# A two-block transformer on one core: where the halves of weights and their operands begin in SBUF, modulo 512 bytes

## The chip, the core and the metric

One core of a Trainium2 chip runs the whole program in one launch. The metric is the device time of that core in microseconds, shorter is better. Before the change three runs took 3350.55, 3352.53 and 3353.84 us; their median is 3352.53 us.

## What is computed

Two blocks over 512 tokens of 2048 features, in float32. The first projects the normalised input to queries, keys, values and gates, runs a differential attention of 8 heads and a state space branch, and merges both through gates. The second has two layers, each with a neighbourhood attention (6 heads), a dilated attention (6 heads) and an attention to 256 memory tokens (4 heads).

```python
def first_block(x, ...):
    h = rms_norm(x, ln_gain[l]);  proj = h @ w_in[l]
    q, k, v, z_att, u, z_ssm, g_att, g_ssm = jnp.split(proj, splits, axis=-1)
    ...
    merged = (jax.nn.sigmoid(g_att) * (y_att @ w_proj_att[l])
              + jax.nn.sigmoid(g_ssm) * (y_ssm @ w_proj_ssm[l]))
    x = x + merged @ w_out[l]

def second_block(x, mem, ...):
    for l in range(DEPTH_2):
        z = rms_norm_2(x, norm_g[l]) @ w_in[l]
        ...
        mk, mv = jnp.split(mem_n @ w_mem_kv[l], 2, axis=-1)
        ...
        x = x + y @ w_out[l]
    return rms_norm_2(x, final_g)
```

Nearly all the work is in these products with weight matrices.

## The kernel before

**Products in three matmuls.** A float32 operand is split into two halves, high and low, that are each exact in the type float32r, and a product is the sum of three: high by high, high by low, low by high. `mm3` (L174 to L179) issues them; L177, L178 and L179 are the three lines at which nearly every matmul of the trace stands.

```python
    def mm3(self, ps, wh, wl, xh, xl, start, stop):
        mm = self.nc.tensor.matmul
        mm(ps, wh, xh, start=start, stop=False)
        mm(ps, wh, xl, start=False, stop=False)
        mm(ps, wl, xh, start=False, stop=stop)
```

The first operand is loaded into the array as the stationary one (128 columns of 4 bytes: 512 bytes of each partition), the second streams past it as the moving one. In a row of the trace the moving tile stands before the stationary one.

**Weights.** `wunit` (L186) brings a unit of weights, 4 k tiles by 256 columns (512 KB), by a DMA to a tile `raw`, and `split` (L181) makes the halves `hl`: ScalarE casts (L183), VectorE subtracts (L184). There are 3 buffers of each, and the units are issued up to 5000 instructions ahead of their place.

```python
            hl = (pool or self.wh).tile([P, 2, 4, 256], FR, tag="hl", ...)[:, :, :kk, :cw]
            self.split(hl[:, 0], hl[:, 1], raw)
```

**Three kinds of product.** `gemm_t` (L215) makes two tiles [128 columns of weights, 512 tokens]: the halves of weights are stationary and the operand moves, 512 columns. For the memory (`memory_kv`, L333) the same function has 256 tokens and so 256 moving columns. `gemm_tok` (L226) makes tiles [128 tokens, 256 columns of weights]: the operand is stationary and the halves of weights move, 256 columns. Both call `accumulate` (L237), which goes over the k tiles and calls `wunit`. Between the matmuls, steps of attention and of the state space branch are spread (`push`, `tick`).

**Where tiles begin.** Pools are laid one behind the other from the bottom of SBUF (left) or from its top (right). The order and sizes in `__init__` (L116 to L134) put the buffers of `raw` and `hl` at 96 bytes past a multiple of 512 in each partition, the left pools that follow at 160 past one, and the right pools at 480 past one. A slice of an operand begins a multiple of 512 bytes into its tile (128 columns are 512 bytes, a row of 512 tokens 2048, the low half follows the high one by 1024, 2048 or 4096), so all slices of a kind have one place modulo 512:

| operand | pool | before | after |
|---|---|---|---|
| halves of weights, `gemm_t` over 512 tokens | `wh` | 96 | 256 |
| halves of weights, `gemm_t` over the memory | `wh` | 96 | 64 |
| halves of weights, `gemm_tok` | `wh` | 96 | 448 |
| the same, last 256 columns of the program | `fin`, right | 480 | 448 |
| operands of the first block's input and last products, and of the second block's output products | `xg1`, `mrg`, `y2`, left | 160 | 0 |
| operands of the memory, of the gated unit, of the merge and of the second block's input products | `memx`, `glu`, `y1`, `xg2`, `xg3`, right | 480 | 0 |

What the text calls the **distance** is how far the stationary tile begins past the moving one, modulo 512:

| kind of product | matmuls | distance before | after |
|---|---|---|---|
| `gemm_t`, 512 columns, operand in a left pool | 4992 | 448 | 256 |
| `gemm_t`, 512 columns, operand in a right pool | 5184 | 128 | 256 |
| `gemm_t`, 256 columns (memory) | 384 | 128 | 64 |
| `gemm_tok`, operand in a left pool (first block's values, last product) | 2112 | 64 | 64 |
| `gemm_tok`, operand in a right pool (memory's and second block's values) | 2688 | 384 | 64 |
| `gemm_tok`, last 256 columns | 192 | 192 | 64 |

The counts are those of the program: 96 matmuls for each `gemm_t` of 16 k tiles, 48 for one of 8.

Of the kernel before, what the change touches and what calls it, by code (L numbers as in the profile page):

```python
# [8 lines left out]
F32 = mybir.dt.float32  # L9
# [7 lines left out]
P = 128  # L17
# [9 lines left out]
# column starts of the first block's input projection  # L27
Q0, K0, V0, ZA0, U0, ZS0, GA0, GS0 = 0, 1024, 2048, 3072, 4096, 5120, 6144, 8192
# column starts of the second block's input projection
# [3 lines left out]
# key tiles that a tile of queries attends to in the neighbourhood attention  # L33
NA_LO = (0, 0, 1, 2)
NA_N = (2, 3, 3, 2)
# the first of the 32 grid columns that it sees
NA_COL = (0, 8, 24, 32)

# instructions by which the loads and splits of weights go ahead of their place
AHEAD = 5000  # L40
AHEAD_FIRST = 180
# k tiles of a product between two steps of other work
# [27 lines left out]
def shape_constants():  # L70
    """Arrays that depend on shapes alone."""
# [10 lines left out]
    # rows of a tile of queries: 16 grid columns by 8 grid rows  # L82
# [27 lines left out]
def natural(ap):  # L110
    """Tokens of a tile in the second block's order, viewed in their natural order."""
    return ap.rearrange("p (c r) -> p r c", r=8)


class Net:
    def __init__(self, ctx, tc, a):  # L116
# [9 lines left out]
        nc.vector.memset(self.onesD, 1.0 / D)  # L126
        self.wr = ctx.enter_context(tc.tile_pool(name="wr", bufs=3))
# [3 lines left out]
        self.col = ctx.enter_context(tc.tile_pool(name="col", bufs=16))  # L131
# [4 lines left out]
    # ---- small helpers  # L136
# [9 lines left out]
    def exact(self, key):  # L146
        """A constant exact in float32r."""
        t, x = self.cp.tile([P, P], FR, name="r_" + key), self.t512(P)
        self.load(x, self.a[key])
        self.nc.scalar.copy(t, x)  # L150
        return t
# [22 lines left out]
    def mm3(self, ps, wh, wl, xh, xl, start, stop):  # L174
        """wh, wl are the exact halves of one operand, xh, xl of the other one."""
# [5 lines left out]
    def split(self, hi, lo, src):  # L181
        """src = hi + lo, both exact in float32r."""
        self.nc.scalar.copy(hi, src)  # L183
        self.nc.vector.tensor_sub(lo, src, hi.bitcast(F32))  # L184

    def wunit(self, src, k0, kk, c0, cw=256, pool=None):  # L186
        with self.tc.high_priority(self.ahead):
            raw = self.wr.tile([P, 4, 256], F32, tag="raw", name=self.nm("raw"))[:, :kk, :cw]
            self.nc.sync.dma_start(out=raw, in_=src[k0 * P:(k0 + kk) * P, c0:c0 + cw].rearrange("(k p) c -> p k c", p=P))
            hl = (pool or self.wh).tile([P, 2, 4, 256], FR, tag="hl", name=self.nm("hl"), bufs=4 if pool else 3)[:, :, :kk, :cw]  # L190
# [3 lines left out]
    def push(self, steps, every):  # L194
        """Spread the steps of a generator over the products that follow: one every so many k tiles,
        or as many as the step before gives."""
# [18 lines left out]
    def gemm_t(self, src, c0, mov, n=T):  # L215
        """Two tiles [128 columns of src, n tokens]; mov: halves [128, 2, n] of each k tile."""
# [7 lines left out]
        return self.accumulate(src, c0, len(mov), out, step)  # L224

    def gemm_tok(self, src, c0, mov, nt):  # L226
        """nt tiles [128 tokens, 256 columns of src]."""
# [7 lines left out]
        return self.accumulate(src, c0, len(mov), out, step)  # L235

    def accumulate(self, src, c0, kt, out, step):  # L237
        """The products over all k tiles; in the first unit of weights the tiles start two by two,
        in the last one they end one after another."""
        n = len(out)  # L240
        for ku in range(0, kt, 4):
            hl = self.wunit(src, ku, 4, c0)
# [10 lines left out]
    def exp_tables(self, after):  # L253
        """Logarithm and exponential from one table, to be loaded after an instruction."""
# [3 lines left out]
    def rsqrt(self, out, ms):  # L258
        """out = (ms + EPS) ** -0.5, a Newton step behind the activation tables."""
# [10 lines left out]
    def norm_stats(self, acc, n=T, pool=None):  # L270
        """acc: squares summed over the k tiles; rstd along the free axis, and as columns."""
# [8 lines left out]
        cols = self.nrm.tile([P, 4], F32, tag="rcol", name=self.nm("rcol"))[:, :n // P]  # L280
# [11 lines left out]
    def add_squares(self, acc, x, first):  # L292
        """acc += x * x"""
# [7 lines left out]
    def gained(self, hl, x, g):  # L301
        """The halves of x * g, g a column."""
# [4 lines left out]
    # ---- the stages  # L307
    def transposed_in(self, src, nt, pool, hls, gains, stage, acc, spill=None):
        """Rows of src to tiles [128 features, tokens] times the gain, and the squares of the rows, in steps."""
# [23 lines left out]
    def memory_kv(self, hls, row, cols):  # L333
        """Keys [features, memory] and values [memory, features] of both layers, to scratch."""
# [16 lines left out]
    def ssm_params(self, sp):  # L351
        """Discretised transition powers and the input and output maps, states on partitions:
        real parts on the lower half, imaginary parts on the upper one."""
# [43 lines left out]
        # powers, doubling  # L397
# [11 lines left out]
        # (a - 1) / lambda  # L409
# [14 lines left out]
        # input maps (re; im) and (-im; re)  # L424
# [18 lines left out]
        # output maps (re; -im) and (-im; -re)  # L443
# [8 lines left out]
        # transition over a chunk for the scan: (ai; -ai), matched to the swapped halves  # L452
# [5 lines left out]
    def ssm_powers(self, e, ar, ai, k0, m1, m2, g0):  # L458
        """e [states, 16 groups, (8 powers, 16 channels)] = ar^k m1 + ai^k m2, in 8 steps."""
# [12 lines left out]
    def ssm(self, sp):  # L472
        """The state space branch from u_d [feature, (j, chunk)] to yl_d, the same order, in steps.
        Tokens are chunk * 8 + j. The powers of a batch of 16 groups go with the products of the one before."""
# [15 lines left out]
        def every(n, k):  # L490
            """The pace of n products, with a step of what goes beside them at every k-th."""
# [92 lines left out]
    # ---- first block  # L584
    def first(self):
# [11 lines left out]
        with ExitStack() as sx:  # L597
# [27 lines left out]
            with tc.tile_pool(name="ssm", bufs=3, side="right", reuse_waits="tile") as sp:  # L625
                # gates of the merge, with the branch between them
# [77 lines left out]
    def residual(self, xp, xg, acc, o, k, gains, spill):  # L704
        """The next layer's operand from a tile of the residual."""
# [6 lines left out]
    def gate(self, ps, row):  # L712
        """silu(ps * row)"""
# [7 lines left out]
    def gated(self, yp, ps, f):  # L721
        """The halves of o * silu(z), o from scratch."""
# [14 lines left out]
    def ssm_out(self, gp, yt, yh):  # L737
        """Tiles of gelu(y + d u) and their halves, in steps."""
# [520 lines left out]
```

## Time and profile before

| | |
|---|---|
| three runs | 3350.55, 3352.53, 3353.84 us |
| profiled execution | span 3350.6 us; no time outside it is listed |
| TensorE busy with matmuls | 3314.5 us, 99% of the span, 17844 |
| VectorE, ScalarE, GpSimd busy | 1754.8, 1175.0 and 293.0 us |
| granted TensorE clock over the span | 0.998 |
| DMA | 122 GB/s in the mean |

Matmuls are pipelined: a row's duration is longer than the step to the next one (0.39 us against some 0.23 us for 512 columns), so durations and busy shares hardly tell how fast TensorE goes. How many matmuls start in a stretch does: a window's length by their number is the **step**. A window also counts the one or two matmuls that began before it and reach into it, and the step is worked out without two of them.

### The profile page before, as it was taken

To read this page: it belongs to the slowest core of one execution; us is meant where nothing else is said; L and a number is where in the kernel's file an instruction comes from. 1 tells how busy PE (TensorE), PEld (TensorE's weight loads), DVE (VectorE), ACT (ScalarE), POOL (GpSimd) and SP (SyncE) were. 2 spreads that over 40 slices of the span, in tenths; PEclk is the share of its full clock that TensorE was granted. 3 is DMA by queue.
4 is the path that set the end of the run, shared out by engine and by line. 5 is a ranking of instruction groups with operands and counts; after the bars stand their busy time and mean duration, and the time that the engine had idled before them with its cause. 6 is when DMAs were issued, how large, how long until landed. Compare 5 with 4: busy or idle time off the path is not lost.

```text
span 3350.6 us, 44958 instructions
## 1 busy us (share of the span) xinstructions
PE 3314.5 (99%) x17844; PEld 2830.3 (84%) x17844; DVE 1754.8 (52%) x3227; ACT 1175.0 (35%) x1851; POOL 293.0 (9%) x426
## 2 busy tenths in 40 slices
PE   8999999999999999999999999999999999999998
PEld 6998877888888788888888888888888888888898
DVE  5564486445888754444444556443354445554433
ACT  4432222243555432233333334323343333342333
POOL 3200001311111000011011000001100100000000
PEclk9999999999999999999999999999999999999999
DMA  6564434453333354344232222333443222223433
GB/s 224 175 195 119 128 121 121 138 190 121 104 101 101 112 174 144 123 145 144 96 95 94 90 85 73 125 118 133 145 134 98 93 89 89 82 92 119 139 111 114
DMA packets 365954, 410.11 MB, mean 122 GB/s; under 512 B 36506, under 2 KB 327209, under 8 KB 365616
## 3 DMA queue, kind: packets, MB, share of 16 engines
q1 hardware_dynamic: 350800, 363.73, 34.2%
q0 software_dynamic: 14944, 43.52, 4.0%
q8 instruction: 140, 2.29, 0.3%
q14 instruction: 70, 0.57, 0.1%
HBM read 355.86 MB, written 47.70 MB: 120 GB/s over the span
## 4 chain that ended last, share of the span: by engine, by line
PE 94%; DVE 3%; DMA 1%; issue 1%; ACT 0%; POOL 0%; SPq 0%; DVEq 0%; ACTq 0%; POOLq 0%
PE pg L177 29%; PE pg L179 28%; PE pg L178 28%; PE pa L178 1%; PE pa L1124 1%; PE pa L177 1%; PE pa L179 1%; DVE hl L184 1%; DVE s L558 0%; PE pa L576 0%; DMA raw<-in_w_in_dram 0%; DVE s L557 0%; DVE s L559 0%; DVE st L560 0%; DVE s L556 0%
## 5 line engine op out<-in xcount | busy, mean ns | idle before, releaser
L184 DVE TENSOR_TENSOR hl<-raw,hl 128x1024 fp32r<-128x1024 f32 x552 | 680.8, 1234 | 965.2 <-ACT hl L183 963.9
L177 PE MATMUL pg<-xg,hl 128*128 128x512 f32 (+1 forms) x2688 | 1077.8, 401 | 0.0
L179 PE MATMUL pg<-xg,hl 128*128 128x512 f32 (+1 forms) x2688 | 1047.5, 390 | 8.2 <-DVE hl L184 8.2
L178 PE MATMUL pg<-xg,hl 128*128 128x512 f32 (+1 forms) x2688 | 1044.9, 389 | 0.0
L183 ACT CAST hl<-raw 128x1024 fp32r<-128x1024 f32 x552 | 578.7, 1049 | 1105.0 <-PE pg L179 933.2
L179 PEld LDWEIGHTS pg<-xg,hl 128*128 128x128 f32 x2688 | 506.0, 188 | 123.3 <-DVE hl L184 13.0
L177 PEld LDWEIGHTS pg<-xg,hl 128*128 128x128 f32 x2688 | 507.5, 189 | 93.4 <-DVE v L305 1.3
L178 PEld LDWEIGHTS pg<-xg,hl 128*128 128x128 f32 x2688 | 507.8, 189 | 87.7
L177 PE MATMUL pg<-hl,xg 128*128 128x256 f32 x1152 | 328.7, 285 | 0.0
L179 PE MATMUL pg<-hl,xg 128*128 128x256 f32 x1152 | 324.0, 281 | 0.0
L178 PE MATMUL pg<-hl,xg 128*128 128x256 f32 x1152 | 323.4, 281 | 0.0
L177 PE MATMUL pg<-yh,hl 128*128 128x512 f32 x576 | 227.1, 394 | 0.0
L179 PE MATMUL pg<-yh,hl 128*128 128x512 f32 x576 | 226.6, 393 | 0.0
L178 PE MATMUL pg<-yh,hl 128*128 128x512 f32 x576 | 225.6, 392 | 0.0
L178 PEld LDWEIGHTS pg<-hl,xg 128*128 128x128 f32 x1152 | 217.3, 189 | 1.5
L177 PEld LDWEIGHTS pg<-hl,xg 128*128 128x128 f32 x1152 | 217.1, 188 | 1.5
L179 PEld LDWEIGHTS pg<-hl,xg 128*128 128x128 f32 x1152 | 216.9, 188 | 0.0
L184 DVE TENSOR_TENSOR wt<-pa,wt 128x512 fp32r<-128x512 f32 (+3 forms) x144 | 83.0, 576 | 120.8 <-ACT wt L183 120.5
L177 PE MATMUL pg<-hl,yh 128*128 128x256 f32 x512 | 144.4, 282 | 0.0
L178 PE MATMUL pg<-hl,yh 128*128 128x256 f32 x512 | 142.2, 278 | 0.0
L179 PE MATMUL pg<-hl,yh 128*128 128x256 f32 x512 | 142.2, 278 | 0.0
L183 ACT CAST wt<-pa 128x512 fp32r<-128x512 f32 (+3 forms) x144 | 71.3, 495 | 169.5 <-PE pa L1124 168.8
(282 smaller groups left out, 3982.9 us busy)
## 6 DMA issues: line engine op xcount, KB each, us to landing
raw<-in_w_in_dram SPq DMA_DIRECT2D x384, 512.0 KB, 3.6
raw<-in_w_out_dram SPq DMA_DIRECT2D x96, 512.0 KB, 3.6
raw<-in_w_mem_kv_dram SPq DMA_DIRECT2D x32, 512.0 KB, 4.3
o_d<-t POOLq DMA_DIRECT2D x40, 256.0 KB, 2.3
t<-o_d SPq DMA_DIRECT2D x40, 256.0 KB, 3.9
sg_d<-t POOLq DMA_DIRECT2D x32, 256.0 KB, 2.5
raw<-in_w_proj_att_dram SPq DMA_DIRECT2D x16, 512.0 KB, 3.9
raw<-in_w_proj_ssm_dram SPq DMA_DIRECT2D x16, 512.0 KB, 3.6
```

What stands on the lines that cost most here:

```text
L177: mm(ps, wh, xh, start=start, stop=False)
L178: mm(ps, wh, xl, start=False, stop=False)
L179: mm(ps, wl, xh, start=False, stop=stop)
L183: self.nc.scalar.copy(hi, src)
L184: self.nc.vector.tensor_sub(lo, src, hi.bitcast(F32))
L1124: self.nc.tensor.transpose(pt[:, i * P:(i + 1) * P], w, self.ident)
```

## The change

It gives `wunit` a parameter `at`, the place of the halves in a tile that is 512 bytes larger (2176 words instead of 2048), and `accumulate` hands it on: 256 for `gemm_t`, 64 for `gemm_t` over the memory, 448 for `gemm_tok`. The rest makes pools begin at multiples of 512: 88 words of filling among the constants (`fill`), the pool of columns `col` moved ahead of the weights' pools, the two small tiles `rcol` moved to it from `nrm`, and a tile of 120 words (`line`) at the top, ahead of the right pools. Comments and docstrings are gone too, which shifts line numbers by 6 to 9.

```diff
+AT_T, AT_MEM, AT_TOK = 256, 64, 448
...
         nc.vector.memset(self.onesD, 1.0 / D)
+        self.col = ctx.enter_context(tc.tile_pool(name="col", bufs=16))
+
+        line = ctx.enter_context(tc.tile_pool(name="line", bufs=1, side="right"))
+        line.tile([P, 120], F32, name="line")
         self.wr = ctx.enter_context(tc.tile_pool(name="wr", bufs=3))
         self.wh = ctx.enter_context(tc.tile_pool(name="wh", bufs=3))
         self.tmp = ctx.enter_context(tc.tile_pool(name="tmp", bufs=8))
         self.nrm = ctx.enter_context(tc.tile_pool(name="nrm", bufs=2))
-        self.col = ctx.enter_context(tc.tile_pool(name="col", bufs=16))
...
-    def wunit(self, src, k0, kk, c0, cw=256, pool=None):
+    def wunit(self, src, k0, kk, c0, cw=256, pool=None, at=0):
...
-            hl = (pool or self.wh).tile([P, 2, 4, 256], FR, tag="hl", name=self.nm("hl"), bufs=4 if pool else 3)[:, :, :kk, :cw]
+            hl = (pool or self.wh).tile([P, 2176], FR, tag="hl", name=self.nm("hl"), bufs=4 if pool else 3)
+            hl = hl[:, at // 4:at // 4 + 2048].rearrange("p (h k c) -> p h k c", h=2, k=4)[:, :, :kk, :cw]
...
-        return self.accumulate(src, c0, len(mov), out, step)
+        return self.accumulate(src, c0, len(mov), out, step, AT_MEM if n == NMEM else AT_T)
...
-        return self.accumulate(src, c0, len(mov), out, step)
+        return self.accumulate(src, c0, len(mov), out, step, AT_TOK)
...
-            hl = self.wunit(src, ku, 4, c0)
+            hl = self.wunit(src, ku, 4, c0, at=at)
...
-        cols = self.nrm.tile([P, 4], F32, tag="rcol", name=self.nm("rcol"))[:, :n // P]
+        cols = self.col.tile([P, 4], F32, tag="rcol", name=self.nm("rcol"), bufs=2)[:, :n // P]
...
-            hls = [self.wunit(w_out, ku, 4, f * P, pool=fp) for ku in range(0, KD, 4)]
+            hls = [self.wunit(w_out, ku, 4, f * P, pool=fp, at=AT_TOK) for ku in range(0, KD, 4)]
...
         self.lam = cp.tile([P, 1], F32, name="lam")
+        cp.tile([P, 88], F32, name="fill")
```

No instruction is added, removed or moved: on each of the five engines both programs have the same operations on the same tiles in the same order. Of the waits two differ, because buffers of one stage now lie over others of the stage before: one addition of GpSimd (the bias of a neighbourhood attention) no longer waits for TensorE, and the load of the final gain (`fg`, in `last`) also waits for a matmul of the second layer's attention.

## Rows read from the trace of the kernel before

**Rows 1.** The page: span, busy time of the matmul engine, granted clock, the last chain.
```profile
span 3350.6 us, 44958 instructions
PE 3314.5 (99%) x17844; PEld 2830.3 (84%) x17844; DVE 1754.8 (52%) x3227; ACT 1175.0 (35%) x1851; POOL 293.0 (9%) x426
...
PEclk9999999999999999999999999999999999999999
...
PE 94%; DVE 3%; DMA 1%; issue 1%; ACT 0%; POOL 0%; SPq 0%; DVEq 0%; ACTq 0%; POOLq 0%
```

**Rows 2.** Groups by shape, whole span (count, busy us, mean ns), a third of each kind.
```profile
L177 PE MATMUL pg<-xg,hl 128*128 128x512 f32 x2560 | 1041.7, 407 | 0.0
...
L177 PE MATMUL pg<-hl,xg 128*128 128x256 f32 x1152 | 328.7, 285 | 0.0
...
L177 PE MATMUL pg<-yh,hl 128*128 128x512 f32 x576 | 227.1, 394 | 0.0
...
L177 PE MATMUL pg<-hl,yh 128*128 128x256 f32 x512 | 144.4, 282 | 0.0
...
L177 PE MATMUL pg<-m,hl 128*128 128x512 f32 x256 | 100.9, 394 | 0.0
```

**Rows 3.** Windows of 512-column products alone: stretch, length, matmul time (count), clock, DMA.
```profile
1372.00:1532.00 160.00, 160.00 (x701) 1.00 0.42 143
1192.00:1350.00 158.00, 158.00 (x682) 1.00 0.50 159
2100.00:2245.00 145.00, 145.00 (x626) 1.00 0.37 120
2995.00:3135.00 140.00, 140.00 (x604) 1.00 0.37 121
212.20:257.20 45.00, 45.00 (x195) 1.00 0.59 169
```

**Rows 4.** Windows of 256-column products alone, the same columns.
```profile
144.00:166.00 22.00, 22.00 (x188) 1.00 0.69 223
167.00:188.80 21.80, 21.80 (x186) 1.00 0.65 215
1650.00:1672.00 22.00, 22.00 (x186) 1.00 0.30 94
...
3318.00:3339.80 21.80, 21.80 (x187) 1.00 0.32 99
```

**Rows 5.** Timeline, first block's values: first and last of 83 matmuls (start, duration).
```profile
833.69 0.28 PE L177 MATMUL pg<-hl,xg 128*128 128x256 f32 x1
...
842.99 0.28 PE L178 MATMUL pg<-hl,xg 128*128 128x256 f32 x1
```

**Rows 6.** Timeline, last product: first and last of 83 matmuls.
```profile
3195.69 0.36 PE L177 MATMUL pg<-hl,yh 128*128 128x256 f32 x1
...
3205.09 0.28 PE L178 MATMUL pg<-hl,yh 128*128 128x256 f32 x1
```

**Rows 7.** Timeline, all engines, 1430 us: a moving stream and the next load.
```profile
1430.03 0.39 PE L178 MATMUL pg<-m,hl 128*128 128x512 f32 x1
1430.04 0.19 PEld L179 LDWEIGHTS pg<-m,hl 128*128 128x128 f32 x1
```

**Rows 8.** Window of the scan (busy and count by engine), and matmuls' wait in it.
```profile
428.00:536.00 108.00, 100.47 (x429) 79.48 (x427) 100.71 (x362) 21.22 (x26) 7.45 (x11) 1.00 0.38 117
...
PE pg L179 <- DVE hl L184: 7.5, 9, 1.1
```

**Rows 9.** What feeds a unit of weights: groups by line, DMA landing, load of `fg`.
```profile
L184 DVE TENSOR_TENSOR hl<-raw,hl 128x1024 fp32r<-128x1024 f32 x552 | 680.8, 1234 | 965.2 <-ACT hl L183 963.9
L183 ACT CAST hl<-raw 128x1024 fp32r<-128x1024 f32 x552 | 578.7, 1049 | 1105.0 <-PE pg L179 933.2
raw<-in_w_in_dram SPq DMA_DIRECT2D x384, 512.0 KB, 3.6
3151.35 0.42 SPq L154 DMA_DIRECT2D fg<-in_final_g_dram  x1
```

More of the change, by code (lines that the diff above doesn't have):

```diff
@@ L233, in step, with accumulate @@
             self.mm3(out[i], x[:, 0, t], x[:, 1, t], hl[:, 0, kk], hl[:, 1, kk], first, last)
-        return self.accumulate(src, c0, len(mov), out, step)
-    def accumulate(self, src, c0, kt, out, step):
+        return self.accumulate(src, c0, len(mov), out, step, AT_TOK)
+    def accumulate(self, src, c0, kt, out, step, at):
         n = len(out)
         for ku in range(0, kt, 4):
-            hl = self.wunit(src, ku, 4, c0)
+            hl = self.wunit(src, ku, 4, c0, at=at)
             order = [(k, i) for k in range(4) for i in range(n)]
```

## The prediction

> **What bounds the kernel now.** I read the page first: TensorE is busy with matmuls 99% of the span, the chain that ended last is PE for 94%, and the granted clock is nine tenths or more of full speed in every slice, the 2.4 GHz level [rows 1]. So a change that moves no instruction can only show in how fast matmuls follow each other, and the durations do not tell that: 512 columns are listed with some 394 to 407 ns [rows 2] though the next one starts after about 230. The step has to be read from windows with nothing but one kind of product in them.
>
> For 512 columns the operand in a left pool (distance 448) gives 160 us / 699 = **228.9 ns**; the operand in a right pool (distance 128) gives 158 / 680 = 232.4, 145 / 624 = 232.4 and 140 / 602 = 232.6, so **232.4** [rows 3]. Same engine, shape, clock and line; in each of these windows TensorE never idles. One stretch with distance 448 stands at 45 / 193 = 233.2 [rows 3]: the same places can also settle in a slower rhythm. For 256 columns the distance 64 gives 9.30 us / 82 = **113.4** [rows 5] and, in the last product where each run restarts behind transposes, 9.40 / 82 = 114.6 [rows 6]. Distance 384 gives 22.0 / 186 = 118.3 and 22.0 / 184 = 119.6, the memory's products at 128 give 21.8 / 184 = 118.5, the last columns at 192 21.8 / 185 = 117.8 [rows 4]. The window with 118.3 moves over twice as many bytes as that with 119.6 [rows 4], so the DMA traffic is not what makes the difference; the distance goes with it. A mechanism that fits: the load of the next stationary tile begins 0.01 us after a moving stream begins and lasts 0.19 us [rows 7], so the two reads of SBUF run side by side, and where they begin to each other can cost the stream a few ns.
>
> **The change, part by part.** I sum against the profiled execution, 3350.6 us, 1.9 below the median of the runs.
>
> *256 columns.* After the change all of them stand at distance 64, which the trace shows; I take 114.0, between its two steps [rows 5, 6]. The 2688 matmuls at 384 are now at 118.9 (between 118.3 and 119.6): 2688 x 4.9 ns = 13.2 us. The memory: 384 x 4.5 = 1.7 us. The last 192: x 3.8 = 0.7 us. Together **15.6 us**. Their places modulo 512 change (moving at 448 instead of 96), the distance does not; that only the distance counts is what this term assumes. At the ends: at 113.4 it is 17.5 us, and if the place counts too and they stay near 118.5, it is about 1 for what is moved, and 2112 x (118.5 - 114.0) = 9.5 us is lost on those that now stand well.
>
> *512 columns.* 10176 matmuls (three lines of 2560 + 576 + 256 [rows 2]) go to distance 256, which no window shows. Below, the stream cannot be faster than a column per cycle: 512 / 2.4 GHz = 213.3 ns at the clock of the rows [rows 3]. Above, the slow rhythm of 233.2 is the worst settled step [rows 3]; one more such delay (the slow 256-column step is 118.5 to 120 where the clear one is 113.4, so about 6 ns) would be 239. Between these I take **226.7**, twice the clear 256-column step of 113.4 [rows 5]: the same bytes stream past, and the 228.9 at distance 448 shows that 512 columns can come within 2 ns of it. Why the clear value at 256: if reads that meet in the same part of a 512-byte period are what costs, then half a period is the start from which they are farthest apart on both sides. It is a guess, and a row speaks against its simple form: for 256 columns the clear distance is 64, not the farthest one. The sum: 5184 x (232.4 - 226.7) = 29.5 us, 4992 x (228.9 - 226.7) = 11.0 us. Of the second, 429 matmuls lie in the scan, where VectorE is busy 100.7 of 108 us and TensorE already waits for its halves [rows 8]; what they gain (0.9 us) is waited for instead. So **39.6 us**.
>
> A rule speaks against all of this. The rows: steps of 113.4 and 118.3 to 119.6 for the same 256 columns, with a stationary load beside each [rows 4, 5]. The Trainium skill (TensorE: Matmul & The Clock Gate, Part 2, Step-by-step, on LDWEIGHTS) says that TensorE has two independent read ports and that loading the next tile's weights takes no read bandwidth from the running matmul. By that rule the distance changes nothing and the time stays; by the rows it costs 5 ns. The trace differs from the rule as far as it goes, and I follow the rows.
>
> *The rest* costs nothing. Casts, subtractions and DMAs work on tiles of the same size; a unit of weights takes ScalarE 1.05, VectorE 1.23 and its transfer 3.6 us [rows 9], while TensorE uses it up in 24 x 226.7 ns or 48 x 113.4 ns = 5.4 us; only the memory's units go in 24 x 114 ns = 2.7 us, where the 0.65 to 0.69 DMA share [rows 4] has room for 4% more. If that cover went, the loss is bounded by the memory's own gain. The load of `fg` waits for a matmul of the attention that ends before the window at 2995 [rows 3]; it is issued at 3151 [rows 9], so the wait has long ended and nothing queues behind it. The wait that GpSimd loses is of an engine with 9% load [rows 1].
>
> The sum: 3350.6 - 15.6 - 39.6 = 3295.4, and 1.9 more for the median of the runs: **3297 us**.
>
> **Rivals.**
> *Half of it.* At distance 256 the step is 228.9, as at 448: only the right pools gain, 5184 x 3.5 = 18.1 us. 3352.5 - 15.6 - 18.1 = 3319 us. For it: 448 is the best settled step that 512 columns show. Against: nothing but that 256 has not been seen.
> *Only the 256 columns.* The new distance is like the mean of the two old ones (230.7): 3337 us.
> *No effect.* The rule above holds, and steps differ by something that goes with the stages (their traffic, their interleaved steps): 3352 us. Against: windows of different traffic at one distance agree within 1% [rows 3, 4].
> *Slower.* Distance 256 is a bad one and 512 columns settle at 233.2 everywhere: 5184 x 0.8 + 4992 x 4.3 = 25.6 us lost, 15.6 won, 3362 us; at 239 it is 3422. It decides from 10176 matmuls at a step of about 232.2, where the loss equals the 15.6. For it: that rhythm has been seen, and two of the three settled steps lie above 232.
> *Far faster.* The old places all begin 32 bytes past a multiple of 64, and the new ones at one. If that is a part of each stream's extra time, steps fall below any seen; a further 6.7 ns, as between 233.2 and 226.7, gives 10176 x 6.7 = 68 us more, 3229 us. Nothing in the rows shows an even place, for or against. The Trainium skill (the same page, Back-to-back issue gap) has 216 ns for 512 columns of bf16; by it the 512 columns would give back 149 us in all, an estimate that no row here supports.
>
> **How the numbers follow.** Forecast 0.45, half of it 0.23, only the 256 columns 0.10, no effect 0.04, slower 0.10, far faster 0.08. A difference under about 0.2% (6.7 us) can't be told from none. Faster by more are the first three and the last, 0.86; within it no effect, 0.04; slower 0.10. The range leaves out the slower case and the far faster one, and goes from 3275 (two more ns per 512 columns than forecast) to 3353 (no effect at all). The forecast's own range is 3285 to 3308, for steps of 225.5 to 227.8.
>
> **What would show it.** In the profile after, the windows of 512 columns in left and right pools must have one and the same step, near 226.7; the values of the second block and the memory's products 113 to 115; the last columns 114 instead of 117.8. PE stays at 99%, the scan stays bound by VectorE, and counts of instructions do not change. Wrong would be a step of 512 columns above 230, different steps in left and right pools (then it is not the distance alone), a first block's or last product's `gemm_tok` that is slower than 114.6, or a new wait of matmuls for `hl`.

## The result and the profile after

| | before | changed |
|---|---|---|
| median of the runs of one comparison | 3352.85 us (4 runs) | 3313.28 us (4 runs, 3310.74 to 3314.32) |
| ratio, 95% interval | | 0.9882 [0.9868, 0.9896] |
| profiled execution: span | 3350.6 us | 3312.3 us |

The change wins 39.6 us; 55.5 were forecast. The page of the changed kernel, with the rows that answer to [rows 1]:

```profile
span 3312.3 us, 44959 instructions
PE 3275.6 (99%) x17844; PEld 2823.8 (85%) x17844; DVE 1753.0 (53%) x3227; ACT 1174.2 (35%) x1851; POOL 293.3 (9%) x426
...
PEclk9999999999999999999999999999999999999999
```

The same instructions, the same clock, the same busy engines, and 38.3 us less: matmuls follow each other more closely. The line of mm3 that waited for halves in the scan [rows 8] does so as before, and it is still the only wait for weights. The row is of the whole span (us in all, times, longest), where the kernel before has 8.2 us in 10 waits:

```profile
PE pg L185 <- DVE hl L190: 8.8, 10, 1.1
```

The windows with 512 columns alone, which answer to [rows 3] (stretch, length, matmul time and count, clock, DMA share, GB/s). The second has its operand in a left pool, the first, third and fourth in a right one, the fifth is the stretch in a left pool that stood at 233.2:

```profile
1180.00:1338.00 158.00, 158.00 (x698) 1.00 0.53 167
1360.00:1520.00 160.00, 160.00 (x707) 1.00 0.45 145
2080.00:2225.00 145.00, 145.00 (x642) 1.00 0.38 124
2960.00:3100.00 140.00, 140.00 (x620) 1.00 0.38 121
210.00:254.00 44.00, 44.00 (x197) 1.00 0.59 175
```

158 / 696 = 227.0, 160 / 705 = 227.0, 145 / 640 = 226.6, 140 / 618 = 226.5, 44 / 195 = 225.6: one step in left and right pools. A count over a window is only good to a matmul or so; the starts of single matmuls are better. The first and the last of 1823 matmuls that follow each other without a break, with operands of left and of right pools (start, duration):

```profile
1124.96 0.40 PE L183 MATMUL pg<-xg,hl 128*128 128x512 f32 x1
...
1537.97 0.39 PE L184 MATMUL pg<-xg,hl 128*128 128x512 f32 x1
```

413.01 us / 1822 = **226.7 ns**, the forecast value to its last digit.

The 256 columns do not do what was forecast. (A run, from here on, is a sequence of matmuls of one kind that nothing breaks.) Timeline of the changed kernel, first and last matmul of a run each: a value product of the memory (191 matmuls), one of the first block (the run of [rows 5], 83), a value product of the second block (191), and a long run of the last product (83, as in [rows 6], but one group of columns later; all its long runs go alike):

```profile
188.19 0.29 PE L183 MATMUL pg<-hl,xg 128*128 128x256 f32 x1
...
209.74 0.28 PE L184 MATMUL pg<-hl,xg 128*128 128x256 f32 x1
...
827.17 0.28 PE L183 MATMUL pg<-hl,xg 128*128 128x256 f32 x1
...
836.71 0.28 PE L183 MATMUL pg<-hl,xg 128*128 128x256 f32 x1
...
1634.45 0.28 PE L183 MATMUL pg<-hl,xg 128*128 128x256 f32 x1
...
1656.83 0.28 PE L184 MATMUL pg<-hl,xg 128*128 128x256 f32 x1
...
3178.30 0.36 PE L183 MATMUL pg<-hl,yh 128*128 128x256 f32 x1
...
3188.04 0.28 PE L184 MATMUL pg<-hl,yh 128*128 128x256 f32 x1
```

21.55 / 190 = 113.4, but 9.54 / 81 = 117.8, 22.38 / 190 = 117.8 and 9.74 / 82 = 118.8. All four stand at distance 64 with the same places, the second and fourth had this distance before the change as well and went at 113.4 and 114.6 [rows 5, 6]. The first step of a run behind transposes takes 0.20 us, which is what lifts 117.8 to 118.8 here and 113.6 to 114.6 in [rows 6]. So there are **two rhythms at distance 64**, 113.3 and 117.8: over the unbroken runs of at least 20 matmuls (no step above 130 ns) of this trace the means are 113.4 to 114.2 or 117.7 to 117.8, and nothing in between.

Where the time went, summed over the trace from the start of each matmul to the start of the next one (waits included):

| matmuls | count | before, us | changed, us | won | forecast |
|---|---|---|---|---|---|
| 512 columns | 10176 | 2406.8 | 2374.8 | 32.0 | 39.6 |
| 256 columns, distance 384 before | 2688 | 323.9 | 316.3 | 7.6 | 13.2 |
| 256 columns, memory | 384 | 45.6 | 44.5 | 1.1 | 1.7 |
| 256 columns, first block's values | 768 | 89.4 | 90.7 | -1.3 | 0 |
| 256 columns, last product with its last columns | 1535 | 182.0 | 185.3 | -3.3 | 0.7 |
| all others (attention, transposes, state space) | 2292 | 287.0 | 285.2 | 1.8 | 0 |

Together 37.9 of the 38.3 us. The 256 columns give 4.1 us where 15.6 were forecast. That the whole gain is 39.6 us, the very figure that was forecast for the 512 columns alone, is chance.

### The profile page after: what moved, and what is told of

Read it like the earlier page. It is cut to its first block, busy times and chain, and to the rows that moved or that the text cites. A ratio compares the mean times of both kernels' runs of the same rounds, so it can differ in the third digit from the quotient of the medians.

```text
span 3312.3 us, 44959 instructions
## 1 busy us (share of the span) xinstructions
PE 3275.6 (99%) x17844; PEld 2823.8 (85%) x17844; DVE 1753.0 (53%) x3227; ACT 1174.2 (35%) x1851; POOL 293.3 (9%) x426
## 4 chain that ended last, share of the span: by engine, by line
PE 94%; DVE 3%; DMA 1%; issue 1%; ACT 0%; POOL 0%; SPq 0%; ACTq 0%; DVEq 0%; POOLq 0%
PE pg L183 29%; PE pg L185 28%; PE pg L184 28%; PE pa L1132 1%; PE pa L184 1%; PE pa L185 1%; PE pa L183 1%; DVE hl L190 1%; PE pa L584 0%; DVE s L565 0%; DVE s L566 0%; DVE s L567 0%; DVE st L568 0%; DVE s L564 0%; PE pa L779 0%
## 5 line engine op out<-in xcount | busy, mean ns | idle before, releaser
L189 ACT CAST hl<-raw 128x1024 fp32r<-128x1024 f32 x552 | 578.9, 1050 | 1074.5 <-PE pg L185 890.5
L190 DVE TENSOR_TENSOR wt<-pa,wt 128x512 fp32r<-128x512 f32 (+3 forms) x144 | 83.1, 577 | 118.2 <-ACT wt L189 117.7
```

## The experiments

Two questions were open: does the distance set the step, or the place; and what decides between the two rhythms. All kernels start from the changed one.

### Every pool 160 bytes further, distances of the products as they are

```diff
-        line.tile([P, 120], F32, name="line")
+        line.tile([P, 80], F32, name="line")
...
-        cp.tile([P, 88], F32, name="fill")
+        cp.tile([P, 128], F32, name="fill")
```

> The changed kernel with every pool, left and right, 160 bytes further on: all distances as in the changed kernel, but moving operands at 160 and the weights of the 256-column products at 96, the very places that the first block's values and the last product had before the change. Theory A (the distance alone sets which rhythms are open, and how a run of matmuls begins picks one of them): 512 columns at 226.7, the runs of the last product at 118.8 as in the changed kernel, time 3313 within 7. Theory B (the place modulo 512 counts too): the last product goes back to its 114.7 of before, some 1200 matmuls by 4 ns = 5 us faster, 3308, or the 512 columns leave 226.7.

3312.64 us (3311.52 to 3313.57), ratio 0.9883 [0.9868, 0.9898], no different from the changed kernel. Its window in the left pool, and the run of the last product, which has the very places of before (moving at 96, stationary at 160):

```profile
1360.00:1520.00 160.00, 160.00 (x708) 1.00 0.43 142
```
```profile
3174.39 0.36 PE L183 MATMUL pg<-hl,yh 128*128 128x256 f32 x1
...
3184.13 0.28 PE L184 MATMUL pg<-hl,yh 128*128 128x256 f32 x1
```

160 / 706 = 226.6 with every place moved: for the step the distance counts, not the place, and that the new places are multiples of 64 is worth nothing. And 9.74 / 82 = 118.8 where the kernel before had 114.6 at the same places and distance: the slow rhythm of this run does not come from where its own tiles stand.

One distance is not as in the changed kernel, against what the expectation says. The transposes that break the last product read the unit matrix, which lies ahead of the filling and stays where it is, while their other operand moves by 160: they go from 384 to 384 + 160 = 32 modulo 512, the distance of the kernel before. And which runs are fast did change: of the 72 runs of the second block's values with at least 18 matmuls, 16 have the other rhythm. What that tells stands with the three tries below.

### One kind of product alone

The 512 columns at 256 and the 256 columns at their old distances (first kernel); the reverse (second kernel). `at_tok` and `at_t` are set, stage by stage, to the place that gives the old distance.

```diff
-        return self.accumulate(src, c0, len(mov), out, step, AT_TOK)
+        return self.accumulate(src, c0, len(mov), out, step, self.at_tok)
...
```
```diff
-        return self.accumulate(src, c0, len(mov), out, step, AT_MEM if n == NMEM else AT_T)
+        return self.accumulate(src, c0, len(mov), out, step, AT_MEM if n == NMEM else self.at_t)
...
```

> Pools at multiples of 512, 512-column products at distance 256 as in the changed kernel, but every 256-column product at the distance that it had before (64, 384, 192, 128). By the trace the 512 columns are worth 36 us and the 256 columns some 4 us: 3317. By the terms of the prediction (39.6 and 15.6): 3313 and thus no slower than the changed kernel only if its 256 columns gave nothing. If place and not distance counts, the 256-column steps differ from those of the kernel before (118.3 to 119.6 at 384).

> Pools at multiples of 512, 256-column products at distance 64 as in the changed kernel, but 512-column products at the distances of before (448 with operands of left pools, 128 with those of right pools). By the prediction's term (15.6 us): 3337. By the trace of the changed kernel, where most 256-column runs stand at 117.8: 3349 (3345 to 3352). The 512-column steps should be 228.9 and 232.4 again if the distance alone counts; if the place counts, others.

512 columns alone: 3321.75 us, ratio 0.9909 [0.9894, 0.9924], 31.0 us won. 256 columns alone: 3345.36 us (10 runs), ratio 0.9979 [0.9970, 0.9989], 7.4 us. The first is slower than the 3317 that was expected of it; the second lies between its two, the 3337 of the prediction's term and 3349, just inside the range of the latter. Together 38.4 against the change's 39.6: within the spread the two gains add. The traces show that they are not independent. With the 512 columns changed alone, the second block's values (distance 384) and the last product (distance 64, not touched):

```profile
1634.47 0.28 PE L184 MATMUL pg<-hl,xg 128*128 128x256 f32 x1
...
1657.26 0.28 PE L185 MATMUL pg<-hl,xg 128*128 128x256 f32 x1
...
3161.40 0.36 PE L184 MATMUL pg<-hl,yh 128*128 128x256 f32 x1
...
3171.14 0.28 PE L185 MATMUL pg<-hl,yh 128*128 128x256 f32 x1
```

22.79 / 190 = 119.9 as before [rows 4], but 9.74 / 82 = 118.8 where before had 114.6 at the same distance [rows 6]. With the 256 columns changed alone, the same two runs, both at 64:

```profile
1644.34 0.28 PE L184 MATMUL pg<-hl,xg 128*128 128x256 f32 x1
...
1665.89 0.28 PE L185 MATMUL pg<-hl,xg 128*128 128x256 f32 x1
...
3184.36 0.36 PE L184 MATMUL pg<-hl,yh 128*128 128x256 f32 x1
...
3193.76 0.28 PE L185 MATMUL pg<-hl,yh 128*128 128x256 f32 x1
```

21.55 / 190 = 113.4 and 9.40 / 82 = 114.6: here the forecast's step is there. These runs have the places and distances of the changed kernel, where they go at 117.8 and 118.8; only the 512 columns elsewhere differ. So what sets the rhythm of a run at distance 64 lies outside the run, in what ran ahead of it. And since runs that the first kernel leaves at distance 64 turned slow in it, the 512 columns' own gain is more than its 31.0 us: by the starts, their time falls from 2406.8 to 2372.9 us, 33.9 less.

### All distances in one program

The place of the weights goes round with a counter of products, so neighbouring products of one program stand at different distances: multiples of 64 (twice, in two orders), odd multiples of 32, and places off any multiple of 32.

```diff
-        return self.accumulate(src, c0, len(mov), out, step, AT_MEM if n == NMEM else AT_T)
+        self.nt_ += 1
+        k = self.nt_
+        return self.accumulate(src, c0, len(mov), out, step, 64 * (k % 8))
...
```

> Pools at multiples of 512; the place of the halves goes on by 64 bytes from each product to the next, so that every product kind runs through all eight distances. Theory A: 512 columns 226.7 at 256, 228.9 (or 233.2) at 448, 232.4 at 128 although the places differ from those of before; 256 columns 113.4 or 117.8 at 64, 117.8 at 192, 118.3 to 120 at 384. For the forecast's guess that the farthest start is best: 512-column steps grow from distance 256 to both sides, worst at 0. Its rival (no order in it): the worst is somewhere else. Time between 3313 and 3365, the mean of good and bad distances.

> The same eight distances as in the first sweep, in another order and so with other products, stages and neighbours at each. If the distance sets the step, 512 columns again stand at 226.7 for 0 and 256, 233.3 for 64 and 320, 232.5 for 128 and 384, 228.9 for 192 and 448, within 0.3 ns but for runs in the slow rhythm; if the steps of the first sweep went with the stages, they move. For 256 columns: 0 and 256 at 120.0, 128 and 384 at 118.5 to 120.0, 192 and 448 at 117.8; 64 and 320 at 113.3 or 117.8. If 320 has the fast rhythm alone, all its runs are at 113.3 to 113.6; if it is the same as 64, some are at 117.8.

> The distances 32, 96, 160, 224, 288, 352 and 416, product after product. Theory A (the step depends on the distance modulo 256 alone, and the places in between lie between their neighbours or on one of them): for 512 columns 32 and 288 agree within 0.3 ns, as do 96 and 352, 160 and 416; 32 somewhere in 226.7 to 233.3, 96 in 232.4 to 233.3, 160 in 228.9 to 232.5, 224 in 226.7 to 228.9. For 256 columns 32 in 113.3 to 120, 96 in 113.3 to 118.6. Theory B (an odd multiple of 32 bytes costs something of its own): some steps above 233.3 or above 120.

> Distances off the multiples of 32: 4, 8, 16, 24, 48, 240, 248 and 252 for 512 columns, 48, 56, 60, 68, 72, 80, 16 and 240 for 256 columns, product after product. Theory A (reads go in pieces of 64 bytes, and a stream that begins off the other one's multiple of 64 touches a piece more): whatever is not a multiple of 64 behaves as the odd multiples of 32 did, 233.3 to 234.3 for 512 columns and 116.6 to 120 for 256. Theory B (the step changes smoothly with the distance): 4, 8, 248 and 252 stay below 229 for 512 columns; 60 and 68 show the two rhythms of 64, 113.3 and 117.8. A place whose 256-column runs are all below 115 would be worth a kernel of its own.

The four took 3345.68, 3349.72, 3375.02 and 3358.76 us, one run each. The last matmul of each of nine products of 512 columns that follow each other in the first sweep; from one row to the next lies a product of 96 matmuls, and the distances of these eight are 256, 320, 384, 448, 0, 64, 128 and 192:

```profile
2100.10 0.40 PE L186 MATMUL pg<-xg,hl 128*128 128x512 f32 x1
...
2121.88 0.39 PE L186 MATMUL pg<-xg,hl 128*128 128x512 f32 x1
...
2144.28 0.39 PE L186 MATMUL pg<-xg,hl 128*128 128x512 f32 x1
...
2166.59 0.39 PE L186 MATMUL pg<-xg,hl 128*128 128x512 f32 x1
...
2188.56 0.40 PE L186 MATMUL pg<-xg,hl 128*128 128x512 f32 x1
...
2210.34 0.39 PE L186 MATMUL pg<-xg,hl 128*128 128x512 f32 x1
...
2232.74 0.39 PE L186 MATMUL pg<-xg,hl 128*128 128x512 f32 x1
...
2255.05 0.39 PE L186 MATMUL pg<-xg,hl 128*128 128x512 f32 x1
...
2277.02 0.40 PE L186 MATMUL pg<-yh,hl 128*128 128x512 f32 x1
```

Divided by 96: 226.9, 233.3, 232.4, 228.9, then once more 226.9, 233.3, 232.4, 228.9 (the crossing into the product adds some 0.2). **The period is 256 bytes, not 512**, and distance 0 is as good as 256. The second sweep, with other products at each distance, gave the same steps in its clean runs. In the third, in the same way, products at 32, 96, 160 and 224:

```profile
2116.02 0.39 PE L186 MATMUL pg<-xg,hl 128*128 128x512 f32 x1
...
2138.42 0.39 PE L186 MATMUL pg<-xg,hl 128*128 128x512 f32 x1
...
2160.90 0.40 PE L186 MATMUL pg<-xg,hl 128*128 128x512 f32 x1
...
2183.32 0.39 PE L186 MATMUL pg<-xg,hl 128*128 128x512 f32 x1
...
2205.71 0.39 PE L186 MATMUL pg<-xg,hl 128*128 128x512 f32 x1
```

233.3, 234.2, 233.5 and 233.2: all bad, and this kernel is the slowest of all. They do not lie between their neighbours, as its theory A had it (224 stands between 228.9 and 226.7), but 288, 352 and 416 again repeat 32, 96 and 160. In the fourth, products at 248, 252, 48 and 4:

```profile
2127.23 0.40 PE L188 MATMUL pg<-xg,hl 128*128 128x512 f32 x1
...
2149.63 0.39 PE L188 MATMUL pg<-xg,hl 128*128 128x512 f32 x1
...
2171.39 0.39 PE L188 MATMUL pg<-xg,hl 128*128 128x512 f32 x1
...
2193.79 0.39 PE L188 MATMUL pg<-xg,hl 128*128 128x512 f32 x1
...
2216.10 0.39 PE L188 MATMUL pg<-xg,hl 128*128 128x512 f32 x1
```

233.3, **226.7**, 233.3 and 232.4. So 4 bytes to one side cost nothing and 4 bytes to the other 5.7 ns: neither the smooth curve nor the steps of 64 bytes that the expectations had. Distance 16 gave 233.3 in most runs and 226.7 in three, so 512 columns know two rhythms as well, at some distances. Nothing went below 226.7.

The four sweeps together, steps in ns by distance modulo 256 (for 256 columns a single short run can lie some 0.5 ns off):

| distance | 0 | 4 | 8 | 16 | 24 | 32 | 48 | 64 | 96 | 128 | 160 | 192 | 224 | 240 | 248 | 252 |
|---|---|---|---|---|---|---|---|---|---|---|---|---|---|---|---|---|
| 512 columns | 226.7 | 232.4 | 230.7 | 233.3 or 226.7 | 230.0 to 231.3 | 233.3 | 233.3 | 233.3 | 234.2 | 232.4 | 233.3 | 228.9 | 233.3 | 228.3 | 233.3 | 226.7 |
| 256 columns | 119.3 to 120.1 | 118.3 | | 117.2 | | 118.3 | 119.0 | 113.3 or 117.8 | 117.2 to 118.9 | 118.4 to 120.0 | 119.9 | 117.8, a few 113.3 | 116.4 to 117.9 | 113.3 to 118.8 | 117.6 | 120.0 |

At 56, 60, 68, 72 and 80 the 256 columns had 117.1 to 122. The two shapes have different good places: 0 is best for 512 columns and among the worst for 256, and 64, the best mean for 256 (114.9 and 115.3 in the first two sweeps), is a bad one for 512. No distance tried in more than one run leaves 256 columns in the fast rhythm alone.

### The two distances that modulo 256 are the same

```diff
-AT_T, AT_MEM, AT_TOK = 256, 64, 448
+AT_T, AT_MEM, AT_TOK = 0, 64, 448
```
```diff
-AT_T, AT_MEM, AT_TOK = 256, 64, 448
+AT_T, AT_MEM, AT_TOK = 256, 320, 192
```

> The changed kernel with the halves of weights of the products of 512 columns at 0 instead of 256 past a multiple of 512, so that their distance is 0. If the step has a period of 256 bytes: 226.7 ns for 512 columns as with 256, the 256 columns again mostly at 117.8, and 3313 us (3309 to 3317). If half a period of 512 is what is good, as the prediction's reason had it, distance 0 is the worst place, steps are 233 and the time is 3375 us. If what runs ahead picks the rhythm of the 256 columns by its place modulo 512 and not 256, they may now fall into 113.4: 3297 to 3305 us.

> The changed kernel with distance 320 instead of 64 for all products of 256 columns (their halves at 192, the memory's at 320). If the period is 256 bytes in every respect: the same two rhythms, mostly 117.8, and 3313 us (3309 to 3317). If 320 has the fast rhythm of 113.4 alone: 4992 + 384 matmuls at up to 4.3 ns less, 15 to 20 us: 3293 to 3299 us. If the rhythm is a chance of how a run begins: some runs at each, 3300 to 3317 us.

3311.67 us (3310.67 to 3312.41), ratio 0.9879 [0.9862, 0.9895], and 3313.17 us (3311.99 to 3314.18), ratio 0.9883 [0.9869, 0.9898]: both the changed kernel's time, as a period of 256 bytes has it. The prediction's reason for 256 ("half a period is the farthest start") would have made distance 0 the worst. In the first of the two the long runs of the last product are fast without any change to them:

```profile
3175.93 0.36 PE L183 MATMUL pg<-hl,yh 128*128 128x256 f32 x1
...
3185.33 0.28 PE L184 MATMUL pg<-hl,yh 128*128 128x256 f32 x1
```

9.40 / 82 = 114.6, against 118.8 in the changed kernel. There the last product's runs, which two transposes break every 36 matmuls, repeat fast, slow, fast, long slow; here slow, fast, slow, long fast.

### What picks the rhythm: three tries

First the transposes that break the last product: the unit matrix in eight places 32 bytes apart, one for each column group.

```diff
-                        nc.tensor.transpose(pt[:, j * P:(j + 1) * P], xt[j][:, i * P:(i + 1) * P], self.ident)
+                        nc.tensor.transpose(pt[:, j * P:(j + 1) * P], xt[j][:, i * P:(i + 1) * P], ident)
...
```

> The changed kernel, with the unit matrix of the transposes that break the last product into runs copied to eight places, 32 bytes further for each of its column groups, so that the transposes' own distance goes 480, 448, 416, 384, 352, 320, 288. What is asked is what picks the rhythm (113.3 or 117.8) of a run of 256 columns at distance 64. In the changed kernel (transposes at 384) the runs of the last product change between the two at nearly each break, in the kernel before (transposes at 32) all runs but the first and two at the end are fast. Theory A (the transposes' distance sets how a run starts, and so its rhythm): the pattern differs from group to group; at 384 the rhythm changes at each break, at 288 (32 modulo 256) it is the same after each break as ahead of it, and some distance may leave every run fast; 3305 to 3318 us. Theory B (the distance of the transposes does not matter): the same pattern of fast, slow, fast, slow in all seven groups, 3313 us within 3.

3313.67 us in one run. The pattern does differ from group to group (at 384 fast, slow, fast, slow as in the changed kernel, at 416 three fast and a slow one, at 320 slow, slow, fast, fast), so theory B falls; but no distance left all runs fast. The last group, at 288, has too few whole runs to say whether the rhythm stays there.

The other traces answer that for 32, which is the same modulo 256. Take the last product's 23 runs of 35 and 83 matmuls (the first step behind the transposes left out) and the 22 breaks between them. With the transposes at 384 the rhythm changes at every break: 22 of 22 in the changed kernel, in both kernels of one kind alone, with the 256 columns at 320 and in the last try below, 21 of 22 with the 512 columns at 0. With them at 32 it stays: no change in the kernel before, one in the kernel shifted by 160 bytes, which runs nearly all of this product slow where the kernel before runs it fast. In the changed kernel, three breaks in a row:

```profile
3188.28 0.38 PE L978 MATMUL pa<-c_ident,t 128*128 128x128 f32 x2
...
3192.60 0.38 PE L978 MATMUL pa<-c_ident,t 128*128 128x128 f32 x2
...
3197.06 0.38 PE L978 MATMUL pa<-c_ident,t 128*128 128x128 f32 x2
```

36 matmuls and two transposes take 4.32 us, then 4.46. So in this product the breaks turn the rhythm round or keep it by their own distance, and what it is at the entrance decides the rest. A kernel with the new distances that enters this product fast with its transposes at 32 was not run.

Then the low half of the weights at another distance than the high one, so that every third matmul differs.

```diff
-            hl = hl[:, at // 4:at // 4 + 2048].rearrange("p (h k c) -> p h k c", h=2, k=4)[:, :, :kk, :cw]
+            hi, lo = at if isinstance(at, tuple) else (at, at)
+            hl = Halves(*(hl[:, o:o + 1024].rearrange("p (k c) -> p k c", k=4)[:, :kk, :cw] for o in (hi // 4, 1024 + lo // 4)))
...
```

> The changed kernel with the low half of the weights of each product of 256 columns moved on its own, so that of the three matmuls of mm3 the second has another distance than the first and third: 320 for the high half (64 modulo 256) and 288, 256, 224, 192, 160, 128, 96 for the low one, and once 480 and 64, product after product. What is asked: runs that are entered directly from a matmul at some other distance were fast in the sweeps (113.3), and runs entered from products of 512 columns at 256 or 0 were slow (117.8). Theory A (a matmul at another distance puts the stream back into the fast rhythm): a mixture in which every third matmul does so stays below 115.6, the mean of the two rhythms, at all its runs. Theory B (each matmul has the step of its own distance): the means are two thirds of 113.3 to 117.8 and one third of the sweeps' 120.0, 118.6, 117.8, 116.7, so 114.4 to 118.5, and both rhythms are still seen. Time 3308 to 3325 us.

3324.33 us. A miss for both theories: the eight mixtures have means of 117.8 to 119.7 and no run below 117.4. In none of them is the fast rhythm left, in the seven neither that have two matmuls of three at 320: there a single one that stands elsewhere costs it for the other two as well.

Last, the matmuls directly ahead. In the changed kernel all seven runs of 256 columns of at least 49 matmuls that stand right behind a product of 512 columns are slow; with the 512 columns at their old distances six of the seven were fast.

```diff
-            hl = self.wunit(src, ku, 4, c0, at=at)
+            hl = self.wunit(src, ku, 4, c0, at=at if tail is None or ku + 4 < kt else tail)
...
-        xs = [self.scaled_row(ap, ps) for ps in self.gemm_t(w_in, K0 + h0 * P, xg)]
+        xs = [self.scaled_row(ap, ps) for ps in self.gemm_t(w_in, K0 + h0 * P, xg, tail=448)]
...
```

> The changed kernel, with the last unit of weights (24 of 96 matmuls) of seven products of 512 columns at 448 instead of 256: the four key projections of the first block, the first key projection of the neighbourhood attention in each layer, and the last gate of the second layer, which all stand directly ahead of a run of 256 columns. In all kernels with 512 columns at 256 or 0 these runs were slow (117.8), seven of seven in each of them; where the products ahead stood at 448 or 128 and all else was the same, six of the seven were fast. Theory C (the distance of the matmuls directly ahead decides in which rhythm a run starts, and a few of them are enough): the runs of the values near 814, 890, 971, 1051, 1634 and 2512 us have 113.3 to 113.7 now; 659 matmuls by 4.4 ns less 168 by 2.2 ns give 2.5 us, so 3310.8 us, within 3 for what the breaks behind them make of it. Theory D (it takes the whole product, or it is chance): most of the seven stay at 117.8, 3313 us within 3.

3313.17 us (3310.89 to 3313.47), ratio 0.9882 [0.9865, 0.9898]. The first block's second key projection is followed by this run of 50 matmuls, and the second block's values by the one below it:

```profile
889.69 0.28 PE L183 MATMUL pg<-hl,xg 128*128 128x256 f32 x1
...
895.25 0.28 PE L184 MATMUL pg<-hl,xg 128*128 128x256 f32 x1
...
1633.62 0.28 PE L183 MATMUL pg<-hl,xg 128*128 128x256 f32 x1
...
1656.00 0.28 PE L184 MATMUL pg<-hl,xg 128*128 128x256 f32 x1
```

5.56 / 49 = 113.5, and the runs near 970 and 1050 us have the same; in the changed kernel all three have 117.8. But 22.38 / 190 = 117.8 as ever, and the runs near 813 and 3111 us stay slow as well. Three of seven: the distance of the last 24 matmuls ahead can turn a run, and 448 does not turn each. In the second block the products ahead of the sequences at 113.4 had stood at 128, which was not tried. The last product's long runs turned fast by the way (114.6), which neither theory foresaw: its first break led to the rhythm of 113.3 instead of 117.8, and with a change at every break that turns all later ones round. Still the time is the same within its spread.

Chance from run to run is not what decides. Those 72 runs of the second block's values have the same rhythms, one by one, in the changed kernel, in those with 0 and 320, with the eight unit matrices and with the last 24 matmuls at 448.

## Why the prediction was right, and where it was wrong

**What bounds the kernel** held. TensorE at 99%, no instruction moved, no new wait for weights, the scan still bound by VectorE: nearly all of the gain is the step (36.1 of the 38.3 us of the profile).

**512 columns: step right, reason wrong, size somewhat high.** The forecast step of 226.7 stands in every clean window, in left and right pools alike, so "half of it" (228.9), "only the 256 columns", "no effect" and "slower" (233.2) all fell. The value was taken from twice the clear 256-column step, and that came out: 113.3 and 226.7 are the lowest steps of any run at any distance, 272 and 544 cycles at the 2.4 GHz level, one in sixteen more than there are columns. The reason given for why 256 would be clear was wrong, as distances 0, 252 and 256 show; the prediction itself named a row that spoke against it. So that 256 is a clear distance was luck: of the sixteen distances modulo 256 that the sweeps took, two have 226.7 in all their runs. The gain is 32.0 us in this profile and 36.2 in the kernel shifted by 160 bytes, not 39.6: the sum took the differences of the clean windows (5.7 and 2.2 ns) for all 10176 matmuls, and over all steps below 260 ns, interleaved stretches too, the means fell by 4.8 (232.4 to 227.6) and 1.9 (229.5 to 227.6).

**256 columns: the term that was mis-sized.** "After the change all of them stand at distance 64, which the trace shows; I take 114.0, between its two steps [rows 5, 6]." Those two, 113.4 and 114.6, are one rhythm, and the trace of before held a second at that distance. Of its 2016 matmuls in unbroken runs at 64 (20 or more, as above), 334 stand in runs at 117.8, the first run of the first block's values and the first of the last product among them; the rows had been taken from the others. The first of these, first and last of 72 matmuls in the kernel before:

```profile
820.13 0.28 PE L177 MATMUL pg<-hl,xg 128*128 128x256 f32 x1
...
828.50 0.28 PE L179 MATMUL pg<-hl,xg 128*128 128x256 f32 x1
```

8.37 / 71 = 117.9. In the changed kernel 3311 of 5227 go at 117.8. 3311 x (117.8 - 114.0) = 12.6 us, about what the term lacks (15.6 - 4.1 = 11.5). The assumption that the distance alone sets the step is right for which steps are possible, and wrong for which of two a run takes. One of the prediction's own signs of being wrong showed here: runs of the first block and of the last product slower than 114.6.

**That only the distance counts**, and not the place, was right for the possible steps: 3312.64 us with all places moved. So was "far faster" being unlikely: even places gave nothing. One reading against "no effect" does not hold: "windows of different traffic at one distance agree within 1%". At distance 448 the prediction's own windows have 228.9 and 233.2, 1.9% apart.

**The rule of the Trainium skill** (TensorE: Matmul & The Clock Gate, Part 2, Step-by-step: two independent read ports, so that loading the next weights takes no read bandwidth from the running matmul) does not, as the prediction applied it, hold here: by it the distance should change nothing, and one program showed 226.7 to 233.3 for streams of one shape, set apart by where the two operands begin to each other. The measurement decides; what it is in the reads that collides, no run here shows.

**Range and chance.** 3313.28 lies in the range and outside the forecast's own 3285 to 3308. By the time alone "half of it" (3319) is nearer than the forecast (3297); the steps decide against it. The forecast's mechanism is what happened, with both terms too large, the 256 columns' by 11.5 us and the 512 columns' by 7.6.

**What stays open** is what decides between the two rhythms. Shown is that the place and distance of a run itself do not, that it changes with the distances of what runs ahead, that a run keeps its rhythm to the next break, and that in the last product the break turns it round with the transposes at 384 and keeps it with them at 32. Neither the transposes' distance nor that of the last 24 matmuls explains all runs elsewhere. At 4.4 ns for each of the 3311 matmuls the slow rhythm still costs the changed kernel an estimated 14.6 us. No kernel tried beats it by more than the spread; the fastest, 3311.67 us with the 512 columns at 0, has an interval that covers it.

## What to carry to other kernels

When TensorE is the bound and nothing waits, compare the starts of matmuls of one shape across stages: unequal steps at one clock are a lead, and where stationary and moving tiles begin to each other, modulo 256 bytes here, is a cheap thing to try, by a sweep that takes all distances through one program. Put each shape at its own best distance, for the best of one was a bad one for the other. And when a trace shows a good step, look for all runs with the same condition before counting it for thousands of instructions: the 334 matmuls at distance 64 that went at 117.8 were there to be read.

## What the runs showed that was not expected

- The period of 256 bytes: 226.9, 233.3, 232.4 and 228.9, twice over in eight neighbouring products.
- The lopsided best place: 252 and 0 give 226.7 for 512 columns, 4 gives 232.4 and 248 gives 233.3.
- Two sharp rhythms at one distance, 113.3 and 117.8, which a run takes up within its first few matmuls and keeps: a run of 191 has one or the other throughout.
- Edits to some products change the rhythm of others that they do not touch: with the 256 columns changed alone the last product's long runs go at 114.6, with the 512 columns changed as well at 118.8.
- A short break can turn the rhythm round or leave it: in the last product at all or all but one of 22 breaks with the transposes at distance 384, at none or one with them at 32.
